# Delta-rule block inverses: 32x32 substitution against 16x16 substitution joined by TensorE products, with a new order of the woven streams

## The chip, the cores and the metric

The kernel runs on one core of one Trainium2 chip. The metric is the device time of one execution in microseconds, the median of the runs that are shown. The engines are named as in the profile: PE (TensorE, products), PEld (its weight loads), DVE (VectorE), ACT (ScalarE), POOL (GpSimd) and SP (SyncE, which issues nearly all DMAs of this kernel).

## What is computed

Two layers of a diffusion backbone over 512 latent tokens with 256 context tokens, 1024 features, everything in float32. Layer 0 mixes tokens in two ways side by side, neighbourhood attention (8 heads of 64) and a gated delta rule in both directions (4 heads of 128); layer 1 mixes with a gated spatial unit. Each is followed by a squared-ReLU MLP. The delta rule is the part at hand. The kernel works with blocks of 128 tokens (2 of context, 4 of latent tokens), in which the reference does this:

```python
kk = jnp.einsum('nbhrd,nbhjd->nbhrj', kb, kb)
lmat = jnp.where(strict, bb[..., :, None] * kk * decay, 0.0)
rhs = jnp.concatenate([bb[..., None] * vb, (bb * eg)[..., None] * kb], axis=-1)
sol = lax.linalg.triangular_solve(lmat, rhs, left_side=True, lower=True, unit_diagonal=True)
u_v, w_k = sol[..., :dv], sol[..., dv:]
...
def step(S, xs):
    u_v_n, w_k_n, aqk_n, qg_n, kdec_n, gl_n = xs
    u = u_v_n - jnp.einsum('bhck,bhkv->bhcv', w_k_n, S)
    o = jnp.einsum('bhck,bhkv->bhcv', qg_n, S) + jnp.einsum('bhcj,bhjv->bhcv', aqk_n, u)
    S = gl_n[..., None, None] * S + jnp.einsum('bhck,bhcv->bhkv', kdec_n, u)
    return S, o
```

The kernel forms the inverse Z of the unit triangular matrix of each block instead of solving, and applies it in the scan. Per pair of heads (a group g, 0 or 1) there are 6 blocks, 2 heads and 2 directions: 24 matrices of 128x128.

## The kernel before

**Products.** A float32 product is made of three: each operand is split into a rounded part and the rest (`whi` and `wlo` for weights, `hh` and `hl` for activations), and `mm3` (lines 134 to 136) issues hi·hi, hi·lo and lo·hi into one PSUM tile. Small products of the delta rule and of attention run in plain float32. Weights come as tiles of 512 KB, one after the other, from `wall` (line 79, and line 521 in layer 0); ACT rounds them, and POOL or DVE makes the rest.

**The woven stage.** `start` (manual order) computes the modulation, the norm and the first three projection tiles. Then `even_mixer` hands 33 generators, the streams, to `weave` (lines 451 to 481). A stream emits some instructions and yields an engine with an assumed duration. `weave` keeps one clock for each of PE, ACT, DVE and POOL and always resumes the stream whose time is the earliest; times up to PE's clock count as equal, and among equals the first in the list wins. So the list is an order of priority. What comes out is one fixed program order for each engine and for SP, and each engine works its queue in that order. Streams wait for each other through events (`signal`, `wait`) and for buffers through tokens (`take`, `give`); tags name buffers: `pd`, `pt`, `pg` in PSUM, `c`, `y`, `g`, `k`, `h`, `a` in SBUF.

The streams that matter here: `dense` projects the 26 tiles that `start` leaves over (PSUM tile `pl` for latent tokens, `pc` for context); `dn_keys`, `dn_values`, `dn_queries` convolve, normalise, rotate and transpose; `dn_matrices(g)` forms the strictly triangular N of each block (line 897) and stores it in `nd` (line 904); `dn_base(g)` inverts the diagonal 32x32 blocks; `dn_inverses(g)` joins them to 64 and to 128 in 6 steps; `dn_scan(g)` runs the recurrence over the steps, and scan 1 waits for scan 0; `dn_outputs` and `dn_finish` make the outputs; `att_keys`, `att_values`, `att_queries` store attention's operands to DRAM; `att_heads` loads a head's operands (`khh`, `kll`, `kcc`, `qhl`: lines 1314 and 1315) when four `k` or four `h` buffers are free; four `attention` lanes work 32 units of 128 queries (lines 1337 to 1377, the last writes `oat`); `ada_woven` makes later modulations on DVE; `out_first` starts the output projection.

**`dn_base` before** puts the 96 diagonal 32x32 blocks of a group on 112 partitions (forward ones on 0 to 47, backward ones on 64 to 111, which are transposed on the way in), and substitutes row by row, 31 rows, the m-th with a product and a reduction over m x m elements on each partition:

```python
for r in range(30, -1, -1):
    m = 31 - r
    nc.vector.tensor_tensor(out=tmp[:, 0:m, 0:m], in0=Z[:, r + 1:32, r + 1:32].rearrange("p j c -> p c j"),
                            in1=nb[:, r, r + 1:32].unsqueeze(1).to_broadcast([112, m, m]), op=ALU.mult)
    nc.vector.tensor_reduce(out=Z[:, r, r + 1:32], in_=tmp[:, 0:m, 0:m], axis=AX.X, op=ALU.add)
```

These are lines 932 and 935 (`zt<-zs,nb` and `zs<-zt` in the profile). A transposed copy follows (938), then 4 stores to DRAM (941, 942) and 24 loads (955) that bring the blocks into `zb`, in the layout of the joins: `zq`, `zn` and `zt`.

**`dn_inverses` before.** A step loads the off-diagonal parts of N (`nm`: lines 979 to 983), lets POOL place the blocks on the diagonals of W and Z (line 990, by a product with the mask `lmask`), multiplies N by W on PE (1009), copies to SBUF on ACT (1011), multiplies by the narrow `zn` (1014), and DVE copies the off-diagonal 32-blocks into Z (1018). The second half of a step (1024 to 1044) joins 64-blocks in the same manner; line 1024 transposes Z on PE. The scan applies Z in line 1112.

## Time and profile before

| | us |
|---|---|
| median of 3 runs (1743.1 to 1745.63) | 1744.21 |
| the profiled execution, its own time | 1746.16 |
| its span, first to last instruction | 1744.3 |
| PE busy (94% of the span) | 1640.8 |
| DVE busy (57%) | 1001.1 |
| ACT busy (35%) | 615.1 |
| POOL busy (14%) | 241.3 |

Busy time counts how long an engine had an instruction in work. PE's instructions overlap, so PE can be called busy and still be slow: the granted clock (PEclk) is given as a share of 2.4 GHz, and 0.5 is 1.2 GHz. The woven stage lies between about 85 us and 537 us of the span.

### The profile page before, as it was taken

What the parts mean: (1) busy time and instruction counts of PE and PEld (TensorE: products, weight loads), DVE (VectorE), ACT (ScalarE), POOL (GpSimd) and SP (SyncE); (2) the same over time, 40 slices, a digit from 0 to 9 for tenths busy, and PEclk for the clock granted to TensorE, in tenths of its full rate; (3) what the DMA queues carried; (4) which work ended last, traced back from release to release, by engine and by line L of the source; (5) the groups of instructions that cost most, each with busy time, mean ns of one, the idle gap of its engine ahead of it and who ended that gap; (6) DMA issues with size and microseconds to landing.
All of it is one profiled execution on the core that took longest, in us unless ns stands there. A gap on an engine that the chain in (4) does not pass through costs nothing.

```text
span 1744.3 us, 23500 instructions
## 1 busy us (share of the span) xinstructions
PE 1640.8 (94%) x8845; PEld 1393.5 (80%) x8845; DVE 1001.1 (57%) x2082; ACT 615.1 (35%) x1002; POOL 241.3 (14%) x215
## 2 busy tenths in 40 slices
PE   7889887969888999999999999999999999999997
PEld 4678776858877888888888999888888888888886
DVE  7876999655756865566646334535444744234433
ACT  4575342336532542123324332323223443123321
POOL 3433344535202100000002000000000200000000
PEclk9999998989879999999999999999999999999999
DMA  9147553676754355555542323232222233233322
GB/s 335 39 131 215 188 171 94 183 215 205 201 170 132 133 193 193 187 188 194 188 137 74 95 86 122 85 97 85 86 87 93 65 105 97 97 97 97 97 87 71
DMA packets 122182, 236.19 MB, mean 135 GB/s; under 512 B 38178, under 2 KB 60114, under 8 KB 122068
## 3 DMA queue, kind: packets, MB, share of 16 engines
q1 hardware_dynamic: 121780, 234.51, 42.1%
q8 instruction: 70, 1.15, 0.3%
q14 instruction: 44, 0.36, 0.1%
q10 hardware_dynamic: 288, 0.17, 0.0%
HBM read 212.59 MB, written 22.04 MB: 135 GB/s over the span
## 4 chain that ended last, share of the span: by engine, by line
PE 78%; DVE 13%; issue 2%; ACT 2%; DMA 2%; SPq 1%; POOL 1%; DVEq 0%; ACTq 0%; POOLq 0%
PE po L134 10%; PE po L135 10%; PE po L136 10%; PE pf L135 9%; PE pf L136 9%; PE pf L134 9%; PE pv L1703 3%; PE pv L1704 3%; PE pv L1705 3%; DVE zt L932 2%; PE tP L1374 2%; DVE junk L334 2%; PE pm L1736 1%; DVE zs L935 1%; PE S L1343 1%
## 5 line engine op out<-in xcount | busy, mean ns | idle before, releaser
L86 ACT CAST whi<-wraw 128x1024 fp32r<-128x1024 f32 x203 | 213.0, 1049 | 642.5 <-PE po L135 355.3
L87 DVE TENSOR_TENSOR wlo<-wraw,whi 128x1024 fp32r<-128x1024 f32 x189 | 231.6, 1225 | 323.1 <-ACT whi L86 305.0
L135 PE MATMUL pf<-nl,whi 128*128 128x512 f32 (+1 forms) x736 | 278.0, 378 | 3.1 <-DVE nl L210 3.1
L136 PE MATMUL pf<-nh,wlo 128*128 128x512 f32 (+1 forms) x736 | 276.8, 377 | 0.9 <-POOL wlo L87 0.9
L134 PE MATMUL pf<-nh,whi 128*128 128x512 f32 (+1 forms) x736 | 277.1, 378 | 0.1
L134 PE MATMUL po<-mh,whi 128*128 128x512 f32 (+1 forms) x544 | 207.5, 381 | 0.0
L136 PE MATMUL po<-mh,wlo 128*128 128x512 f32 (+1 forms) x544 | 207.4, 381 | 0.0
L135 PE MATMUL po<-ml,whi 128*128 128x512 f32 (+1 forms) x544 | 207.2, 381 | 0.0
L87 POOL TENSOR_TENSOR wlo<-wraw,whi 128x1024 fp32r<-128x1024 f32 x14 | 33.4, 2383 | 1148.8 <-ACT whi L86 1141.9
L135 PEld LDWEIGHTS pf<-nl,whi 128*128 128x128 f32 x736 | 138.7, 188 | 28.8 <-DVE nl L210 4.3
L136 PEld LDWEIGHTS pf<-nh,wlo 128*128 128x128 f32 x736 | 138.4, 188 | 25.6 <-POOL wlo L87 1.0
L134 PEld LDWEIGHTS pf<-nh,whi 128*128 128x128 f32 x736 | 138.1, 188 | 24.6 <-ACT whi L86 0.3
L134 PEld LDWEIGHTS po<-mh,whi 128*128 128x128 f32 x544 | 102.0, 187 | 22.3
L135 PEld LDWEIGHTS po<-ml,whi 128*128 128x128 f32 x544 | 102.0, 187 | 22.2
L136 PEld LDWEIGHTS po<-mh,wlo 128*128 128x128 f32 x544 | 101.9, 187 | 22.0
L1704 PE MATMUL pv<-whi,nl 128*128 128x256 f32 x384 | 108.3, 284 | 1.6 <-DVE nl L210 1.6
L1703 PE MATMUL pv<-whi,nh 128*128 128x256 f32 x384 | 108.0, 284 | 1.1 <-ACT nh L209 1.1
L1705 PE MATMUL pv<-wlo,nh 128*128 128x256 f32 x384 | 108.1, 283 | 0.0
L1592 DVE SCALAR_TENSOR_TENSOR xr<-po,gt,xr 128x512 f32<-128x512 f32 (+1 forms) x54 | 37.1, 690 | 115.0 <-PE po L136 114.9
L134 PE MATMUL pl<-hh,whi 128*128 128x512 f32 x232 | 97.9, 422 | 4.4 <-DVE ycv L570 2.6
L528 POOL TENSOR_TENSOR wlo<-wraw,whi 128x1024 fp32r<-128x1024 f32 x31 | 77.9, 2515 | 161.3 <-ACT whi L526 158.4
L135 PE MATMUL pl<-hl,whi 128*128 128x512 f32 x232 | 93.7, 404 | 1.1 <-POOL hl L359 1.1
(373 smaller groups left out, 3121.8 us busy)
## 6 DMA issues: line engine op xcount, KB each, us to landing
wraw<-in_wall_dram SPq DMA_DIRECT2D x237, 512.0 KB
araw<-in_adat_dram SPq DMA_DIRECT2D x80, 512.0 KB
kvt<-kvd SPq DMA_DIRECT2D x24, 256.0 KB
scraw<-in_ada_dram SPq DMA_DIRECT2D x16, 256.0 KB
E<-gd SPq DMA_DIRECT2D x12, 256.0 KB
nd<-N SPq DMA_DIRECT2D x24, 128.0 KB
x<-in_x_dram SPq DMA_DIRECT2D x8, 256.0 KB
shraw<-in_adat_dram SPq DMA_DIRECT2D x4, 512.0 KB
```

Source lines behind the costliest of these rows:

```text
L86: self.nc.scalar.copy(out=hi, in_=w)
L87: (engine or self.split_engine).tensor_tensor(out=lo, in0=w, in1=hi.bitcast(F32), op=ALU.subtract)
L134: self.nc.tensor.matmul(out=out, lhsT=wh, rhs=hh, start=(first and i == 0), stop=False)
L135: self.nc.tensor.matmul(out=out, lhsT=wh, rhs=hl, start=False, stop=False)
L136: self.nc.tensor.matmul(out=out, lhsT=wl, rhs=hh, start=False, stop=(last and i == n - 1))
L334: nc.vector.tensor_tensor_reduce(out=junk, in0=wsh[k][i], in1=row, scale=1.0, scalar=0.0, op0=ALU.mult, op1=ALU.add, accum_out=sa[:, k, i, ...
L528: self.nc.gpsimd.tensor_tensor(out=lo, in0=w, in1=hi.bitcast(F32), op=ALU.subtract)
L932: nc.vector.tensor_tensor(out=tmp[:, 0:m, 0:m], in0=Z[:, r + 1:32, r + 1:32].rearrange("p j c -> p c j"), in1=nb[:, r, r + 1:32].unsqueeze ...
L1592: self.nc.vector.scalar_tensor_tensor(out=self.x[m][:, c0:c1], in0=ps, scalar=gate[:, m:m + 1], in1=self.x[m][:, c0:c1], op0=ALU.mult, op1 ...
L1703: nc.tensor.matmul(out=ps, lhsT=hh, rhs=wh, start=(k == 0), stop=False)
L1704: nc.tensor.matmul(out=ps, lhsT=hl, rhs=wh, start=False, stop=False)
L1705: nc.tensor.matmul(out=ps, lhsT=hh, rhs=wl, start=False, stop=(k == KD - 1))
```

## The change

The substitution stops at 16x16 blocks: `dn_base` keeps both 16-blocks of each 32-block on the same partition, does 15 rows over two m x m squares at once, and stores one array, `zd`. It reads this back in two halves, makes the transposes with DVE's transpose of 32x32 blocks, and joins the 16-blocks to 32x32 with two rounds of 12 narrow products on PE (16 columns each), between them a placing on the diagonals by a DVE product with a mask. The off-diagonal 16x16 parts of N come by 8 loads into `n16`, which is cleared once at the start. ACT and DVE copy the result into `zb`, where 24 loads did it before. N is stored by direction in `nd`, 256 columns a row.

`dn_inverses` places nothing on POOL any more. Z lies in two fixed tiles `zz`, cleared once; POOL clears two 32x32-blocks in each step; the first product takes the narrow `zt`, DVE places its result with the mask `beside32`, and ACT copies the diagonal blocks of Z.

In the planner, many assumed durations are raised, an instruction no longer starts before its stream's own time, the hop between engines is 0.2 instead of 0.15, and DMA issues by the streams go through a helper `dma` that counts 0.45 us of SP's queue for each. The list of streams is in another order. There are 8 `g` buffers instead of 10, 2 `zb` instead of 1, and a smaller DMA scratch. Inverses of group 1 wait in the plan for those of group 0. Left out of the diff below are further changes of assumed durations and calls of `nc.sync.dma_start` that became `self.dma`, the lines that leave `dn_base`, and the old list of streams (both stand in the code above).

```diff
-NSTEP = 8 * (16 * 512 + 16)
+NSTEP = 8 * (16 * 256 + 16)
...
-        hop = 0.15
+        hop = 0.2
         clock = dict.fromkeys("PADG", 0.0)
         self.events = {}
+        self.queue = 0.0
...
+            t = max(t, self.t)
...
             live[best][1] = t + d
+
+    def dma(self, out, in_):
+
+        self.queue = self.t = max(self.queue, self.t)
+        self.queue += 0.45
+        return self.nc.sync.dma_start(out=out, in_=in_)
...
-        ndt = self.dram.tile([6 * NSTEP], F32, name=f"nd{g}")
-        nd = [bass.AP(ndt.tensor, ndt.offset + n * NSTEP, [[512, P], [1, 512]]) for n in range(6)]
+        ndt = self.dram.tile([12 * NSTEP], F32, name=f"nd{g}")
+        nd = lambda t, dd: bass.AP(ndt.tensor, ndt.offset + t * NSTEP + dd * P, [[256, P], [6 * NSTEP, 2], [1, P]])
...
     def dn_base(self, g):
         nc = self.nc
         nd = yield from self.wait(("nd", g))
         for _ in range(3):
             yield from self.take("a")
...
+        mk = lambda n: self.raw.tile([P, 1024], F32, name=n, tag="a")
+        zd = self.dram.tile([96, 1024], F32, name=f"zd{g}")
+        work, Z, spare = mk("nb"), mk("zs"), mk("zt")
+        b16 = lambda t: t.rearrange("p (s a b) -> p s a b", s=2, b=16)
+        nb, tmp, raw = b16(work[0:112, 0:512]), b16(work[0:112, 512:1024]), b16(spare[0:112, 0:512])
+        bw = slice(64, 112)
+        n0 = nd(0, 0)
+        for t, p0, dd, n in ((raw, 64, 1, 48), (nb, 0, 0, 48), (nb, 48, 0, 16)):
+            src = bass.AP(n0.tensor, n0.offset + dd * P, [[32 * 256 + 32, n], [16 * 256 + 16, 2], [256, 16], [1, 16]])
+            self.dma(out=t[p0:p0 + n], in_=src)
         nc.gpsimd.memset(Z, 0.0)
...
+        nc.gpsimd.memset(Z[:, 0:1024:33], 1.0)
         yield "G", 1.0
+        beside = lambda r, c, dd: bass.AP(n0.tensor, n0.offset + dd * P + r * 256 + c, [[256, 16], [NSTEP, 12], [1, 16]])
+        for b in range(0, P, 32):
+            f, e = slice(b, b + 16), slice(b + 16, b + 32)
+            self.dma(out=self.n16[f, :, e], in_=beside(b, b + 16, 0))
+            self.dma(out=self.n16[e, :, f], in_=beside(b + 16, b, 1))
         yield "", 2.0
...
+        nc.scalar.copy(out=nb[bw], in_=raw[bw].rearrange("p s a b -> p s b a"))
+        yield "A", 0.6
+        za = Z[0:112]
+        zd16 = bass.AP(za.tensor, za.offset, [za.ap[0], [528, 2], [32, 16], [1, 16]])
+        for r in range(14, -1, -1):
+            m = 15 - r
+            nc.vector.tensor_tensor(out=tmp[:, :, 0:m, 0:m], in0=zd16[:, :, r + 1:16, r + 1:16].rearrange("p s j c -> p s c j"),
+                                    in1=nb[:, :, r, r + 1:16].unsqueeze(2).to_broadcast([112, 2, m, m]), op=ALU.mult)
+            yield "D", 0.12 + m * m / 480
+            nc.vector.tensor_reduce(out=zd16[:, :, r, r + 1:16], in_=tmp[:, :, 0:m, 0:m], axis=AX.X, op=ALU.add)
+            yield "D", 0.12 + m * m / 480
+        self.dma(out=zd[0:48], in_=Z[0:48])
+        self.dma(out=zd[48:96], in_=Z[bw])
+        yield "", 2.2
+        v = lambda t, o: t[:, o:o + 384].rearrange("p (i t c) -> p i t c", i=2, c=32)
+        w16 = lambda t: t.rearrange("p (i t c) -> p i t c", i=2, c=16)
+        d0, d1, t0, t1 = v(work, 0), v(work, 384), v(spare, 0), v(spare, 384)
+        zt16, zn16 = w16(work[:, 768:960]), w16(spare[:, 768:960])
+        for o, dd in ((d0, 0), (t1, 1)):
+            for i in range(2):
+                src = bass.AP(zd.tensor, zd.offset + (2 * dd + i) * 24 * 1024, [[32, P], [4096, 6], [1, 32]])
+                self.dma(out=o[:, i], in_=src)
+        yield "", 2.5
+        fl = lambda t: t.rearrange("p i t c -> p (i t c)")
+        nc.vector.transpose(out=fl(t0), in_=fl(d0))
+        nc.vector.transpose(out=fl(d1), in_=fl(t1))
+        yield "D", 1.0
+        a, b = slice(0, 16), slice(16, 32)
+        nc.vector.tensor_tensor(out=zt16, in0=t0[..., a], in1=t1[..., b], op=ALU.add)
+        nc.vector.tensor_tensor(out=zn16, in0=d0[..., b], in1=d1[..., a], op=ALU.add)
+        yield "D", 0.71
+        yield from self.take("zb")
+        zb = self.pool.tile([P, 1536], F32, name="zb", tag="zb", bufs=2)
+        zq = zb[:, 0:768].rearrange("p (x i t c) -> p x i t c", i=2, x=2, c=32)
+        zn, zt = v(zb, 768), v(zb, 1152)
+        y = yield from self.tp("y16", "pt")
+        y1, y2 = w16(y[:, 0:192]), w16(y[:, 192:384])
+        for i in range(2):
+            for t in range(6):
+                nc.tensor.matmul(out=y1[:, i, t], lhsT=self.n16[:, i * 6 + t], rhs=zt16[:, i, t], start=True, stop=True)
+            yield "P", 1.35
+        h16 = slice(0, 64), slice(64, P)
+        for x in range(2):
+            for h in range(2):
+                nc.scalar.copy(out=zq[h16[h], x], in_=(d1, d0)[(x + h) % 2][h16[h]])
+        yield "A", 2.0
+        for i in range(2):
+            w = Z[:, 0:768].rearrange("p (t s c) -> p t s c", t=6, c=16)
+            nc.vector.tensor_tensor(out=w, in0=y1[:, i].unsqueeze(2).to_broadcast([P, 6, 8, 16]),
+                                    in1=self.beside16.rearrange("p (s c) -> p s c", c=16).unsqueeze(1).to_broadcast([P, 6, 8, 16]),
+                                    op=ALU.mult)
+            yield "D", 0.9
+            for t in range(6):
+                nc.tensor.matmul(out=y2[:, i, t], lhsT=Z[:, t * P:(t + 1) * P], rhs=zn16[:, i, t], start=True, stop=True)
+            yield "P", 1.35
+        for x in range(2):
+            for h in range(2):
+                dd = 1 - (x + h) % 2
+                z = zq[h16[h], x, :, :, (b, a)[dd]]
+                nc.vector.scalar_tensor_tensor(out=z, in0=y2[h16[h]], scalar=self.row16[h16[h], dd:dd + 1], in1=z,
+                                               op0=ALU.mult, op1=ALU.add)
+        yield "D", 1.2
+        self.give("pt")
         for _ in range(3):
...
+            self.give("a")
+        for k in range(4):
+            ks = slice(k * 32, (k + 1) * 32)
+            x = (1, 0, 0, 1)[k]
+            nc.scalar.copy(out=zn[ks], in_=zq[ks, 1 - x])
             for i in range(2):
...
+                nc.vector.transpose(out=zt[ks, i].rearrange("p t c -> p (t c)"), in_=zq[ks, x, i].rearrange("p t c -> p (t c)"))
+        yield "D", 2.4
+        self.signal(("zb", g), (zq, zn, zt), 0.3)
...
         zq, zn, zt = yield from self.wait(("zb", g))
-        zq = zq.rearrange("p i x f -> p (i x) f")
-        bd = self.lmask.rearrange("p (b c) -> p b c", c=32)
-
-        def place(o, z, n):
-            nc.gpsimd.tensor_tensor(out=o.rearrange("p (s b c) -> p s b c", s=n, c=32), in0=z.unsqueeze(2).to_broadcast([P, n, 4, 32]),
-                                    in1=bd.unsqueeze(1).to_broadcast([P, n, 4, 32]), op=ALU.mult)
+        beside = self.beside32.rearrange("p (b c) -> p b c", c=32).unsqueeze(1).to_broadcast([P, 2, 4, 32])
         two = lambda t: t.rearrange("p (i f) -> p i f", i=2)
+        if g > 0:
+            yield from self.wait(("inverses", g - 1))
         N = yield from load(0)
         for t in range(6):
             nxt = (yield from load(t + 1)) if t < 5 else None
-            ts = slice(t * 32, (t + 1) * 32)
             yield from self.take("Z")
-            Z = yield from self.tu("Z", "g")
+            Zv = self.zz[t % 2]
+            for x, b, c in ((0, 3, 2), (1, 2, 3)):
+                nc.gpsimd.memset(Zv[b * 32:(b + 1) * 32, :, x, c * 32:(c + 1) * 32], 0.0)
+            yield "G", 0.3
             W = yield from self.tu("W", "g")
-            place(W[:, 0:256], zt[:, :, ts], 2)
-            yield "G", 0.7
-            place(Z, zq[:, :, ts], 4)
-            yield "G", 1.4
-            Zv = Z.rearrange("p (i x f) -> p i x f", i=2, x=2)
             y = yield from self.tp("y", "pg")
             sl = lambda o, i: slice(o + i * P, o + (i + 1) * P)
             for i in range(2):
-                nc.tensor.matmul(out=y[:, sl(0, i)], lhsT=N[:, 0, i], rhs=W[:, sl(0, i)], start=True, stop=True)
+                nc.tensor.matmul(out=y[:, 32 * i:32 * i + 32], lhsT=N[:, 0, i], rhs=zt[:, i, t], start=True, stop=True)
             yield "P", 0.43
-            nc.scalar.copy(out=W[:, 256:512], in_=y[:, 0:256])
-            yield "A", 0.27
+            nc.vector.tensor_tensor(out=W[:, 256:512].rearrange("p (i b c) -> p i b c", i=2, c=32),
+                                    in0=y[:, 0:64].rearrange("p (i c) -> p i c", i=2).unsqueeze(2).to_broadcast([P, 2, 4, 32]),
+                                    in1=beside, op=ALU.mult)
+            yield "D", 0.42
+            for b in range(4):
+                ps = slice(b * 32, (b + 1) * 32)
+                nc.scalar.copy(out=Zv[ps, :, :, ps], in_=zq[ps, :, :, t].rearrange("p x i c -> p i x c"))
+            yield "A", 1.0
             for i in range(2):
-                nc.tensor.matmul(out=y[:, 256 + 32 * i:288 + 32 * i], lhsT=W[:, sl(256, i)], rhs=zn[:, i, ts], start=True, stop=True)
+                nc.tensor.matmul(out=y[:, 256 + 32 * i:288 + 32 * i], lhsT=W[:, sl(256, i)], rhs=zn[:, i, t], start=True, stop=True)
             yield "P", 0.43
             for x, b, c in ((1, 0, 1), (1, 3, 2), (0, 2, 3), (0, 1, 0)):
                 ps = slice(b * 32, (b + 1) * 32)
                 nc.vector.tensor_copy(out=Zv[ps, :, x, c * 32:(c + 1) * 32], in_=two(y[ps, 256:320]))
-            yield "D", 0.5
+            yield "D", 0.9
...
+        self.signal(("inverses", g))
...
-            yield "P", 0.86
-            self.give("g")
+            yield "P", 0.9
...
-        self.lmask = self.const.tile([P, P], F32, name="lmask")
+        self.beside16, self.beside32 = [self.const.tile([P, P], F32, name=f"beside{n}") for n in (16, 32)]
+        self.row16 = self.const.tile([P, 2], F32, name="row16")
+        self.n16 = self.const.tile([P, 12, P], F32, name="n16")
+        self.zz = [self.const.tile([P, 2, 2, P], F32, name=f"zz{i}") for i in range(2)]
         self.nm = [self.pool.tile([P, 2, 2, P], F32, name=f"nm{i}", tag=f"nm{i}", bufs=1) for i in range(2)]
-        for t in self.nm:
+        for t in self.nm + self.zz + [self.n16]:
             nc.gpsimd.memset(t, 0.0)
         o = P
...
-        count = dict(pd=0, pt=2, pg=0, w=2, whi=3, a=1, h=0, k=0, bm=2, zb=1, Z=2, kv=2, nr=2,
+        count = dict(pd=0, pt=2, pg=0, w=2, whi=3, a=1, h=0, k=0, bm=2, zb=2, Z=2, kv=2, nr=2,
...
+        self.weave([self.weights(), self.dn_finish(0), self.dn_keys(1), self.attention(3, L), self.dn_inverses(0),
+                    self.dn_outputs(1), self.dn_gates(), self.dn_scan(0), self.dn_keys(0), self.dn_values(0), self.dn_values(1),
+                    self.dn_matrices(0), self.dn_base(0), self.dn_scan(1), self.att_keys(), self.release_h(), self.att_values(),
+                    self.att_gates(), self.att_finish(), self.out_first(), self.dn_finish(1), self.dn_base(1),
+                    self.att_queries(), self.attention(2, L), self.dn_queries(1), self.dn_outputs(0), self.dn_queries(0),
+                    self.dn_matrices(1), self.load_residual(), self.attention(0, L), self.attention(1, L), self.dn_inverses(1),
+                    self.att_heads(), self.dense(), self.ada_woven()])
...
-            self.phase(ctx, {"c": 7, "y": 6, "k": 10, "sc": 2, "g": 10, "ar": 2, "tri": 1, "cos": 1, "sin": 1}, {"pd": 3, "pt": 2, "pg": 3})
+            self.phase(ctx, {"c": 7, "y": 6, "k": 10, "sc": 2, "g": 8, "ar": 2, "tri": 1, "cos": 1, "sin": 1}, {"pd": 3, "pt": 2, "pg": 3})
...
-    lm = [(a == b).astype(f)]
+    s, u = i[:, None] // 16, i[None, :] // 16
+    even = (i[:, None] // 16 % 2 == 0).astype(f)
+    lm = [((s ^ 1) == u).astype(f), ((a ^ 1) == b).astype(f), even, f(1) - even]
...
-    nc = bacc.Bacc("TRN2", target_bir_lowering=False, num_devices=1)
+    nc = bacc.Bacc("TRN2", target_bir_lowering=False, num_devices=1, dynamic_dma_scratch_size=1024)
```

## Rows read from the trace of the kernel before

**Rows 1.** The page, busy us of an engine, share of the span, instructions.

```profile
PE 1640.8 (94%) x8845; PEld 1393.5 (80%) x8845; DVE 1001.1 (57%) x2082; ACT 615.1 (35%) x1002; POOL 241.3 (14%) x215
```

**Rows 2.** Busy time by stage: us; PE, PEld, DVE, ACT, POOL; PEclk, DMA share, GB/s.

```profile
85.00:180.00 95.00, 87.72 (x513) 75.38 (x513) 65.82 (x172) 57.54 (x94) 35.89 (x22) 0.98 0.54 168
180.00:300.00 120.00, 97.81 (x526) 82.66 (x525) 113.86 (x224) 40.51 (x68) 44.77 (x32) 0.91 0.50 148
300.00:350.00 50.00, 47.85 (x337) 42.47 (x337) 34.55 (x82) 18.16 (x52) 29.77 (x36) 1.00 0.60 184
350.00:375.00 25.00, 10.48 (x58) 8.76 (x57) 8.76 (x29) 6.05 (x13) 4.89 (x6) 0.73 0.71 202
375.00:455.00 80.00, 77.42 (x593) 71.83 (x592) 52.27 (x186) 42.79 (x107) 39.53 (x58) 1.00 0.73 210
455.00:537.00 82.00, 67.96 (x363) 60.28 (x362) 54.30 (x168) 35.31 (x76) 9.74 (x12) 0.75 0.65 191
537.00:1744.30 1207.30, 1185.44 (x6139) 1007.69 (x6137) 605.07 (x1090) 373.09 (x530) 41.47 (x19) 1.00 0.35 115
```

**Rows 3.** Groups by line, 80 to 660 us: busy us, mean ns, idle before.

```profile
L932 DVE TENSOR_TENSOR zt<-zs,nb 112x1 f32<-112x1 f32 (+30 forms) x62 | 55.3, 892 | 1.3
...
L935 DVE TENSOR_REDUCE zs<-zt 112x1 f32<-112x1 f32 (+30 forms) x62 | 30.9, 499 | 1.3
...
L990 POOL TENSOR_TENSOR Z<-zb,lmask 128x512 f32<-128x512 f32 x12 | 15.7, 1308 | 0.2
```

**Rows 4.** Timeline of PE: start us, us, instruction, idle before and its releaser.

```profile
285.52 0.66 PE L1024 MATMUL y<-ident,Z 128*128 128x128 f32 x2 [7.45 <-DVE Z L1018]
```

**Rows 5.** The substitution: its lines (ns min/median/max, first and last start), timelines of DVE and POOL.

```profile
L932 DVE TENSOR_TENSOR zt<-zs,nb x62: 149/726/3607, 178.8 to 319.1; 112x1 f32<-112x1 f32 x2, 112x4 f32<-112x4 f32 x2, 112x9 f32<-112x9 f32 x2, 112x16 f32<-112x16 f32 x2
L935 DVE TENSOR_REDUCE zs<-zt x62: 154/419/1153, 179.3 to 325.2; 112x1 f32<-112x1 f32 x2, 112x2 f32<-112x4 f32 x2, 112x3 f32<-112x9 f32 x2, 112x4 f32<-112x16 f32 x2
...
205.64 1.01 DVE L932 TENSOR_TENSOR zt<-zs,nb 112x441 f32<-112x441 f32 x1
...
245.87 1.15 DVE L935 TENSOR_REDUCE zs<-zt 112x31 f32<-112x961 f32 x1
...
278.54 2.35 POOL L528 TENSOR_TENSOR wlo<-wraw,whi 128x1024 fp32r<-128x1024 f32 x1 [5.69 <-ACT whi L526]
...
279.15 2.43 DVE L932 TENSOR_TENSOR zt<-zs,nb 112x441 f32<-112x441 f32 x1
```

**Rows 6.** PE's waits, 80 to 660 us; two links of the chain that ended last.

```profile
PE S L1343 <- DMA qhl<-qad: 11.1, 1, 11.1
...
104.79 3.83 DMA E<-gd
...
407.82 0.89 PE ks L1102 x8
```

**Rows 7.** Timeline of SP's DMA issues: start us, us, issue.

```profile
335.57 6.11 SPq L955 DMA_DIRECT2D zb<-zn  x8
...
348.77 0.92 SPq L955 DMA_DIRECT2D zb<-zn  x2
```

**Rows 8.** The first transfer of the heads: ns min/median/max, first and last issue.

```profile
L1314 SPq DMA_DIRECT2D khh<-kad x16: 445/587/656, 359.2 to 484.2; - x16
```

**Rows 9.** Ends of attention units, 455 to 537 us, in the same form.

```profile
L1377 DVE TENSOR_SCALAR oat<-tP,sm x17: 278/284/285, 459.1 to 522.3; 128x64 f32<-128x64 f32 x17
```

**Rows 10.** Prices of like instructions: a group by line; others in the form of rows 5.

```profile
L1178 DVE TENSOR_TENSOR odn<-au,kk 128x256 f32<-128x256 f32 x8 | 3.0, 420 | 5.3 <-PE au L1166 3.9 <-PE pc L135 1.4
...
L1032 ACT COPY W<-y x12: 372/372/373, 288.0 to 452.5; 128x256 f32<-128x256 f32 x12
...
L1014 PE MATMUL y<-zb,W x48: 194/276/402, 277.4 to 447.6; 128*128 128x32 f32 x48
...
L1560 POOL MEMSET nm<- x2: 524/524/524, 0.7 to 1.2; 128x512 f32 x2
```

More of the change, by code (lines that the diff above doesn't have):

```diff
@@ L948, in dn_base @@
-        zq = zb[:, 0:768].rearrange("p (i x f) -> p i x f", i=2, x=2)
-        zn, zt = [zb[:, o:o + 384].rearrange("p (i f) -> p i f", i=2) for o in (768, 1152)]
-        def load(o, z, dd, p0, n):
-            for i in range(2):
-                src = bass.AP(z.tensor, z.offset + (2 * dd + i) * 24 * 1024 + p0 * 32, [[32, n], [4096, 6], [1, 32]])
-                nc.sync.dma_start(out=o[p0:p0 + n, i].rearrange("p (t c) -> p t c", c=32), in_=src)
-        for x in range(2):
-            for half in range(2):
-                load(zq[:, :, x], zc[0], 1 - (half + x) % 2, half * 64, 64)
@@ L1065, in load @@
             for dd in range(2):
[L1066 removed]
+                self.dma(out=kvt[:, dd], in_=self.kv[g][order[dd][t]].rearrange("p (a f) -> p a f", a=2))
             return kvt
@@ L1550, in out_first @@
             self.give("h")
+        self.signal("done")
     def even_mixer(self):
```

243 lines of the change are left out of this document (105 added, 138 removed).

## Prediction

> **What bounds the kernel now.** I read the page first, for the whole. PE is busy for 94% of the span [rows 1], so a change that is not about dense products can win only where PE stands still or runs slowly. The second view, busy time by stage, says where that is [rows 2]. From 537 us on (both MLPs and the gated mixer) PE is busy for 1185 of 1207 us at full clock, and the diff touches nothing there. The first 85 us are the start, untouched but for memsets and constants. The change lives in the woven stage between: 452 us, of which PE is busy for 389. The 63 us of idle PE lie like this: 7 in 85 to 180, 22 in 180 to 300, 2 in 300 to 350, 15 in 350 to 375, 3 in 375 to 455, 14 in 455 to 537.
>
> To that comes the granted clock: 0.91 in the second stage, 0.73 in the fourth, 0.75 in the last. The time at 1.2 GHz is twice what is missing to 1 (22, 14 and 41 us), and work that is done in it at 1.2 GHz would take half as long at 2.4. In the last stage PE is busy for 83% of the time, so some 17 of the 41 us are lost; in the second about 6, in the fourth and the first 2 each. Idle and slow PE together cost **about 89 us of 452**: 9, 28, 2, 16, 3 and 31, stage by stage. That is all that the change can win, less what it adds to PE.
>
> What ends the waits: from 180 to 300 VectorE (DVE) is busy for 114 of 120 us [rows 2], and 86 us in all are the block substitution, lines 932 and 935 [rows 3]. PE's longest stall there shows what this does: the transpose y<-Z at 285.52 waited 7.45 us for the copies of line 1018 [rows 4], which stood in DVE's queue behind substitution steps, one of 2.43 us among them [rows 5]. From 350 to 375 PE waits 11.1 us for qhl, the last transfer of the first attention head [rows 6]. It was issued late: SP had first spent 14 us on 24 issues for zb, eight in 6.11 us and then about 0.46 each, up to 349.7 [rows 7], and the head's first transfer left at 359.2 [rows 8]. After 455 little but attention is left: 17 of its 32 units end there, between 459 and 523 [rows 9], with PE at 1.2 GHz for half of the stage.
>
> **The change part by part.** *Substitution on DVE.* Line 932 takes 0.15 us for one element and 1.01 for 441: 0.15 us and 1.95 ns an element. Line 935 takes 0.15 for one and 1.15 for 961: 1.04 ns an element [rows 5]. Two 16-blocks side by side keep the transposed read, so I keep both prices. Fifteen rows with 2m² elements are 2480 elements instead of 10416: 15 x 0.15 + 4.8 = 7.1 us and 15 x 0.15 + 2.6 = 4.8, so 11.9 a group where rows 3 show 43.1; the transposing copy goes too (1.1, by line 935's 961 elements). New on DVE in each group: two 32x32-block transposes of 384 columns, two adds of 192, two products of 768, four updates of 192 and eight transposes of 192 on 32 partitions. Scaled from 0.42 us for 256 columns [rows 10] they are 0.55, 0.35, 0.95, 0.35 and 0.3 each: 7.5 us. (If a transpose paid line 932's price, 0.9 instead of 0.55, it would be 1 us more; it reads one tensor, so I take the lower.) That makes 19.4 for 44.2: **25 us less a group, 50 in both**. The inverses get one more DVE product of 256 columns in each of 12 steps, 0.42 each: 5 us back. DVE has 148 us of work between 180 and 350; 45 less, and it is no longer full.
>
> The slow forms deserve a second look: 441 elements took 1.01 us at 205.64 and 2.43 at 279.15, while POOL ran wlo from 278.54 to 280.89 [rows 5]. The Trainium skill (SBUF — State Buffer, Who interferes with whom) says that a DVE instruction with two SBUF inputs and a GpSimd instruction that reads SBUF block each other on a shared read interface; this trace agrees. By that rule up to 1.4 us falls on each product that meets a wlo, and with two or three such in a group the saving would be 21 to 23 instead of 25.
>
> *POOL* loses the placing of line 990, 15.7 us for Z [rows 3] and half as much for W, and gets 24 memsets of 128 columns, 0.2 each beside 0.52 for 512 [rows 10]. *ACT* gets four copies of 32 partitions a step (0.25 each beside 0.37 for 256 columns [rows 10]: 12 us) and eight larger ones a group (0.4: 6 us), and loses the 12 copies of line 1011 and half of line 928: some 12 us more. It is busy for 200 of 452 us [rows 2] and hides them; were it full, they would stand in the steps' chain, 1 us a step. *SP*: 33 issues a group (5 loads, 4 stores, 24 for zb) become 17 (3 loads, 8 of n16, 2 stores, 4 reads): at 0.46 that is 7.4 us less a group. The 64-byte rows of n16 are only 1536 a group and land during the substitution, before whose end nobody needs them; without that cover they cost one landing, 3.8 us.
>
> *PE* gets 24 narrow products a group. Four fp32 products of 128 columns run in 0.89 us, as eight instructions [rows 6], and an instruction with 32 columns shows the same 0.28 [rows 10]. So 0.22 each: **10.6 us more PE**; 21 at 1.2 GHz. Were columns what counts it would be under 3, but rows 10 speak for the higher.
>
> *The chain.* Today 30 us pass from the last reduction of group 0 (247.0) to the second inverse product (277.4) [rows 5, 10]. New: a store and a read, each at most a landing like E's 3.83 us [rows 6], transposes and adds 1.8, products 1.3, placing 1, products, placing and products 2.7, updates 1.4, transposes 2.4: some 18 us. And the substitution, 68 us from first to last step because its 43 us stand between other DVE work [rows 5], should take 20 to 25. The inverses of group 0 can begin some 50 us sooner, those of group 1 more; scan 0 ends sooner, and with it come the five k buffers of which the first head needs four.
>
> *At nothing:* memsets of zz and n16 (2.7 us by rows 10, on POOL in its first 16 us, before wlo; later they would delay a wlo by as much), two more constant loads on SP's slack at 37 us, nd stored as two half rows, ten g buffers to eight (Z takes none any more), a second zb, the scratch size, since the page lists hardware queues alone. The planner's new costs move instructions only; an order nearer to the real durations saves stalls like the 7.45 us, which no row prices.
>
> **The sum.** Stage by stage: the early 9 stay; 28 becomes 10, because DVE stops being full; 16 becomes 7, as SP's stretch halves and buffers come sooner but some fetch stays exposed; 31 becomes 19: heads that begin 40 us sooner finish seven more units under other work at 5.3 us each (15 of them in 375 to 455), so that ten remain alone, at 4 us. 18 + 9 + 12 = 39, with 2 for fewer stalls 41, less 10.6: **30 us**. From the profiled 1746.2 us (the span of 1744.3 and 1.9 around it) to 1716; the median of the runs shown lies 2 us lower, so 1714.
>
> **Rivals.** *A, attention spreads wholly.* If scan 0 ends near 300, half of the heads run under projections; the last stage loses 25 of its 31, the fourth 16, the second 22: 63 less 10.6 is 52, so 1692. For it: after 375, with other work beside it, PE idles for only 3 of 80 us. Against: the last heads need the last projections.
>
> *B, the idle only moves.* If the first head still leaves at 359 [rows 8], because its buffers or the order let it no sooner, the projections run out sooner and attention stands alone sooner, at 1.2 GHz. Then the 18 of the second stage are won, the 10.6 paid and some 5 given back: 1742.
>
> *C, slower.* PE takes its queue in order, and the joining sets three new hand-offs a group (products behind adds, then twice behind a placing) and one changed in each of 12 steps on DVE: 18 places where the 7.45 us of rows 4 can come again, 8.5 with a slow start after it. Four cancel the 30; with six it is 1714 + 51 = 1765. For it: DVE keeps other work in its queue. Against: what stood before line 1018 there is now a third as long.
>
> **How the numbers follow.** My forecast (1695 to 1732: PE's 10.6 or 21, all or nothing of the tail's 12) gets 0.50, A 0.20, B 0.15, C 0.15. A measurement of this kernel can tell about 0.2%, 3.5 us, from no change; half of B lies within, 0.08, the rest of B is faster: 0.77 faster, 0.15 slower. The range from 1682 to 1749 leaves out the far part of A and nearly all of C.
>
> **What would show it.** Right: the substitution's lines near 24 us instead of 86, DVE under 85% where it was 95%, inverses that begin before 240, a first S before 340, fewer than 13 units alone, 96 narrow instructions at 0.11 us. Wrong: PE waits of 5 us or more for the joining's DVE steps, a first S after 355, or a last stage whose clock stays at 0.75.

## The result, and the profile after

The changed kernel takes 1720.15 us, median of 4 runs (1719.23 to 1721.98), beside 1743.65 us for the kernel before (4 runs, 1742.96 to 1745.63): a ratio of 0.9865, with a 95% interval of 0.9848 to 0.9882. That is 23.5 us faster, where 30 were forecast. The two profiled executions lie further apart, 1746.16 and 1719.23 us; their spans are 1744.3 and 1717.4, so 26.9 us are to be found in the traces.

The page of the changed kernel, busy us of an engine, share of the span, instructions:

```profile
PE 1641.4 (96%) x8941; PEld 1396.2 (81%) x8941; DVE 965.3 (56%) x2064; ACT 631.8 (37%) x1056; POOL 218.0 (13%) x218
```

PE does as much as in [rows 1] in a shorter span. Busy time by stage of the changed kernel, columns as in [rows 2]. The last projection now ends at 389 us and the woven stage at about 509, so the limits are moved there:

```profile
85.00:180.00 95.00, 86.35 (x489) 73.85 (x490) 63.43 (x161) 57.34 (x93) 33.86 (x21) 0.95 0.54 161
180.00:300.00 120.00, 110.03 (x651) 95.79 (x650) 93.27 (x235) 53.59 (x109) 44.23 (x47) 0.93 0.59 171
...
300.00:350.00 50.00, 48.81 (x323) 43.16 (x321) 36.50 (x111) 17.76 (x47) 16.08 (x21) 1.00 0.84 274
350.00:389.00 39.00, 38.61 (x267) 34.96 (x268) 27.96 (x92) 26.06 (x61) 13.69 (x18) 1.00 0.78 219
389.00:455.00 66.00, 55.26 (x428) 50.72 (x427) 38.26 (x136) 38.00 (x96) 23.62 (x46) 0.95 0.81 230
455.00:509.00 54.00, 51.42 (x323) 46.61 (x323) 31.12 (x99) 21.92 (x55) 8.66 (x10) 0.87 0.31 100
509.00:1717.40 1208.40, 1185.44 (x6135) 1006.77 (x6133) 608.60 (x1100) 374.51 (x532) 39.06 (x18) 0.99 0.34 115
```

The woven stage fell from 452 us to 424; what follows it takes 1208 us, as before. From 180 to 300 us DVE is busy for 78% of the time, where it was 95%. To count both kernels in one way, I take for the loss of a stage its idle PE time and, for the slow clock, busy time x (1 - clock):

| loss of PE, us | before | after |
|---|---|---|
| 85 to 180 | 9.0 | 13.0 |
| 180 to 300 | 31.0 | 17.7 |
| 300 to 375 (after: to 389) | 19.5 | 1.6 |
| from there to the end of the woven stage | 33.6 | 22.8 |
| sum | 93.1 | 55.1 |

So 38 us of loss went, and the stage is 28 shorter: the rest, 358.9 to 368.9, is 10 us of added work on PE. Groups of the changed kernel by line, 80 to 660 us (busy us, mean ns, idle before):

```profile
L952 DVE TENSOR_TENSOR nb<-zs,nb 112x2 f32<-112x2 f32 (+14 forms) x30 | 19.7, 656 | 0.5
...
L955 DVE TENSOR_REDUCE zs<-nb 112x2 f32<-112x2 f32 (+14 forms) x30 | 9.6, 321 | 0.5
...
L986 PE MATMUL y<-nb,n 128*128 128x16 f32 x48 | 5.9, 262 | 0.1
...
L1000 PE MATMUL y<-zt,zs 128*128 128x16 f32 x48 | 5.6, 256 | 0.0
```

The substitution is 29.3 us where [rows 3] have 86.2, and the narrow products are 96 instructions in 11.5 us, 0.12 each. PE's waits in the changed kernel, 80 to 560 us (total us, times, longest):

```profile
PE tvac L590 <- DVE vaTc L1297: 5.4, 2, 3.7
...
PE pu L1170 <- DVE zz L1100: 2.5, 3, 1.3
...
PE y L1081 <- DVE zz L1075: 1.9, 2, 1.3
...
PE y L1071 <- DVE W L1062: 1.5, 3, 0.7
```

The longest is 3.7 us. The wait of 11.1 us for qhl [rows 6] and that of 7.45 us for line 1018 [rows 4] are gone, and the hand-offs from DVE to PE in inverses and scan (the last three rows) cost 6 us in eight waits.

### The profile page after: what moved, and what is told of

It is laid out like the page before. It is cut to its first block, busy times and chain, and to the rows that moved or that the text cites. A ratio compares the mean times of both kernels' runs of the same rounds, so it can differ in the third digit from the quotient of the medians.

```text
span 1717.4 us, 23655 instructions
## 1 busy us (share of the span) xinstructions
PE 1641.4 (96%) x8941; PEld 1396.2 (81%) x8941; DVE 965.3 (56%) x2064; ACT 631.8 (37%) x1056; POOL 218.0 (13%) x218
## 4 chain that ended last, share of the span: by engine, by line
PE 69%; DVE 3%; issue 1%; ACT 0%; POOL 0%; DVEq 0%; ACTq 0%; POOLq 0%
PE po L134 10%; PE po L135 10%; PE po L136 10%; PE pf L135 9%; PE pf L136 9%; PE pf L134 9%; PE pv L1770 3%; PE pv L1771 3%; PE pv L1772 3%; PE pm L1803 1%; PE tP L1431 0%; DVE nl L210 0%; PE st L173 0%; DVE accx L201 0%; DVE modt L208 0%
## 5 line engine op out<-in xcount | busy, mean ns | idle before, releaser
L87 DVE TENSOR_TENSOR wlo<-wraw,whi 128x1024 fp32r<-128x1024 f32 x189 | 231.5, 1225 | 324.8 <-ACT whi L86 306.4
L87 POOL TENSOR_TENSOR wlo<-wraw,whi 128x1024 fp32r<-128x1024 f32 x14 | 33.4, 2384 | 1149.3 <-ACT whi L86 1131.1
L134 PE MATMUL pl<-hh,whi 128*128 128x512 f32 x232 | 102.2, 441 | 2.9 <-DVE ycv L578 2.9
L136 PE MATMUL pl<-hh,wlo 128*128 128x512 f32 x232 | 95.7, 412 | 0.0
```

What stands on the lines that cost most here:

```text
L87: (engine or self.split_engine).tensor_tensor(out=lo, in0=w, in1=hi.bitcast(F32), op=ALU.subtract)
L134: self.nc.tensor.matmul(out=out, lhsT=wh, rhs=hh, start=(first and i == 0), stop=False)
L136: self.nc.tensor.matmul(out=out, lhsT=wl, rhs=hh, start=False, stop=(last and i == n - 1))
```

## The experiments

The kernels ran on three chips, each beside runs of the kernel before, so they are compared by their ratio to it. "To after" is (ratio - 0.9865) x 1743.65 us; an interval is some 3 us to either side, 5 to 7 for e5, e7, e8 and e12; the 3 us of the changed kernel's own ratio come on top.

One thing has to be known before these runs are read: the plan of `weave` is not the last word on the order of instructions. e3, e4, e6 and e10 change no assumed duration, so they have the plan of the kernel that they start from. Their traces still show PE, ACT and DVE working in another order in places, with DVE instructions moved by up to 12 places in e6, 35 in e3 and e10 and 57 in e4; what moves them is not shown. Only e9 (beside the changed kernel) and e11 (beside e8) ran exactly the order of the kernel that they are compared with.

| run | what | median us | ratio (95% interval) | to after, us |
|---|---|---|---|---|
| e1_math_only | new inverses, old order | 1723.41 | 0.9878 (0.9861 to 0.9894) | +2 |
| e2_plan_only | old inverses, new order | 1758.12 | 1.0079 (1.0064 to 1.0094) | +37 |
| e3_dve_back | after, DVE work put back | 1759.95 | 1.0085 (1.0070 to 1.0100) | +38 |
| e4_dve_cut | before, DVE work taken out | 1726.18 | 0.9899 (0.9882 to 0.9916) | +6 |
| e5_dve_back_planned | e3, known to the plan | 1762.99 | 1.0108 (1.0076 to 1.0140) | +42 |
| e6_pe_double | narrow products twice | 1742.60 | 0.9997 (0.9976 to 1.0017) | +23 |
| e7_late_plan | inverses 30 us later in plan | 1715.05 | 0.9847 (0.9805 to 0.9889) | -3 |
| e8_wlo_dve | wlo on DVE | 1704.40 | 0.9771 (0.9741 to 0.9802) | -16 |
| e9_pool_back | POOL's placing put back | 1730.53 | 0.9929 (0.9908 to 0.9950) | +11 |
| e10_sp_back | 16 issues a group put back | 1746.36 | 1.0000 (0.9982 to 1.0019) | +24 |
| e11_wlo_both | e8, and POOL reads the same | 1726.13 | 0.9899 (0.9883 to 0.9916) | +6 |
| e12_wlo_late | e8 and e7 | 1704.19 | 0.9774 (0.9748 to 0.9800) | -16 |

**The inverses or the order?** The diff does two things, and the prediction gave the new order nothing. e1 has the new `dn_base`, `dn_inverses`, buffers and constants under the old list and durations; e2 is its complement. The core of e1 against the changed kernel (the list of streams and the other streams' durations go back in the same way):

```diff
-        hop = 0.2
+        hop = 0.15
...
-        self.queue = self.t = max(self.queue, self.t)
-        self.queue += 0.45
...
-            yield "A", 1.05
+            yield "A", 0.95
```

> The 16x16 substitution with its joining, the new buffers and copies, but the old list of streams, the old assumed durations, the hop of 0.15 and no clock for SP's queue. Theory M (the gain comes from less DVE work in the substitution and a shorter way to the inverses, as the prediction has it): most of the gain is here, 10 to 24 us faster than before, with DVE in 180 to 300 us well under 95%. Theory O (the gain comes from the new order and the planner's truer durations, the substitution only allows it): within 8 us of before, or slower, because the order was found for the old durations.

> The old 32x32 substitution, old inverses and old buffers, with the new list of streams, the raised durations, the hop of 0.2 and the clock for SP's queue. Theory M: less than 8 us faster than before, or slower, because DVE is still full while the substitution runs (86 us of it). Theory O: 10 to 24 us faster than before.

e1 alone is 21 us faster than before, with DVE busy for 75% of the time from 180 to 300 us, and the order adds some 2 us, which the intervals do not part from nothing. The new order with the old inverses is 14 us slower than before. Its two largest waits of PE, 80 to 560 us:

```profile
PE tqT L590 <- DVE qtok L621: 14.2, 1, 14.2
PE y L1032 <- DVE Z L1026: 13.2, 5, 10.4
```

Both are waits for DVE, the second at the place of the 7.45 us of [rows 4], and DVE is busy for 110 of the 120 us from 180 to 300. This fits an order that brings other work forward and meets a DVE that is still full; that it makes the whole 14 us is not shown. Theory O is out.

**DVE's load alone, from both sides.** e3 gives DVE back about as much work as the change took; e4 takes the long rows out of the old substitution and edits nothing else.

```diff
# e3, behind each of the 15 reductions
+            sq = self.cos[0:112, 0:441].rearrange("p (j c) -> p c j", c=21)
+            for _ in range(2):
+                nc.vector.tensor_tensor(out=spare[0:112, 512:953].rearrange("p (c j) -> p c j", c=21), in0=sq, in1=sq, op=ALU.mult)
# e4, before both instructions of a row of the old substitution
+            if m < 16:
# e5: e3, and the plan knows
-            yield "D", 0.12 + m * m / 480
+            yield "D", 2.12 + m * m / 480
```

> The changed kernel in its own order, with two extra DVE products of 441 elements behind each of the 15 substitution steps of a group (about 30 us more DVE work a group, about what the change took away; nobody uses their results). Theory M: most of the gain is lost, 12 to 25 us slower than the changed kernel. Theory O: less than 8 us slower, since the order leaves the time for it.

> The kernel before in its own order, with the substitution's first-long 16 of 31 rows (m of 16 and more) left out, about 35 us less DVE work a group; nothing else moves, the 24 loads into zb and the placing on POOL stay. What it leaves out are rows 0 to 15 of each 32x32 inverse. Theory M: 12 to 25 us faster than before. Theory O: less than 8 us faster.

> As e3_dve_back, but the plan knows of the extra DVE work (2.0 us more assumed in each of the 15 steps), so that the program order is made for it. Theory M1 (what counts is DVE's time: its other work and the inverses come later whatever the order): still 15 us or more slower than the changed kernel. Theory M2 (what counted in e3 was that an order written for short steps met long ones, so that PE stood behind them in its queue): under 8 us slower than the changed kernel, or equal to it.

e4 is 17.6 us faster than before, though its 24 loads and its POOL work stay: the substitution's two lines fell from 86.2 to 19.1 us. The second inverse product of group 0 also comes 20 us sooner (257.0 us instead of 277.4), so e4 alone does not part DVE's time from an earlier inverse; e7 below does.

e3 loses the whole gain and more, but half of its extra work is not where it was meant to be. The extra products need no result of a reduction, and those of group 0 ran long before the substitution. The extra products and the reductions, in the form of [rows 5]; DVE's time with the extra products in two stretches; and busy time from 85 to 130 us, in e3 and then in the changed kernel, columns as in [rows 2]:

```profile
L958 DVE TENSOR_TENSOR zt<-cos x60: 986/1099/3210, 69.1 to 317.8; 112x441 f32<-112x441 f32 x60
...
L955 DVE TENSOR_REDUCE zs<-nb x30: 134/276/622, 200.6 to 316.1; 112x2 f32<-112x2 f32 x2, 112x4 f32<-112x8 f32 x2, 112x6 f32<-112x18 f32 x2, 112x8 f32<-112x32 f32 x2
```

```profile
85.00:130.00 45.00, 30.78 (x23) 0.81 0.23 71
...
180.00:300.00 120.00, 27.90 (x21) 0.90 0.56 159
```

```profile
85.00:130.00 45.00, 29.48 (x169) 24.51 (x169) 44.69 (x70) 22.14 (x39) 12.72 (x5) 0.81 0.23 71
...
85.00:130.00 45.00, 41.28 (x238) 35.34 (x239) 33.93 (x78) 34.56 (x59) 16.04 (x8) 0.96 0.40 129
```

The products took 1.3 us each, not 1.0, 80 us in all, and cost 38. The 30 of group 0 lie between 69 and 128 us, ahead of that group's substitution, whose first reduction comes at 200.6 us instead of 180.3. DVE is full there, and PE's loss from 60 to 130 us, counted as in the table of losses, is 30 us where the changed kernel has 11: about half of the 38. Only the other half stands for the 30 products of group 1, from 250 to 319 us, beside a substitution. In e5, with the work known to the plan, the first 30 lie as early (70 to 128 us) and cost as much there, and the rest is some 23 us: M2 is out, since that rest alone is far above 8 us. So a full DVE holds PE up in either place; that the substitution's stage is where the change gained rests on e4, on e1 beside e2, and on the second half of e3 and e5.

**The way to the inverses.** The prediction priced a shorter chain from the substitution to the first inverse.

```diff
-        self.signal(("zb", g), (zq, zn, zt), 0.3)
+        self.signal(("zb", g), (zq, zn, zt), 30.0)
```

> The joined blocks are signalled 30 us later in the plan (30.0 instead of 0.3), so that the inverses of both groups, and what hangs on them, are put 30 us later into the queues; no instruction is added. Theory C (an early inverse is a part of the gain by itself): 8 us or more slower than the changed kernel. Theory D (DVE's freed time is the gain, and the way to the inverses is short enough either way): within 5 us of the changed kernel.

Not slower: if anything 3 us faster, within its interval. The first inverse product comes at 277.4 us instead of 247.4, but the order then catches up: the sixth step of group 0 begins 7 us later than in the changed kernel and the last of group 1 9 us sooner. So 30 us at the start of the inverses cost nothing as long as the plan knows it, and theory C is out.

**The price of the joining on PE.**

```diff
+                for _ in range(2):
-                nc.tensor.matmul(out=y1[:, i, t], lhsT=self.n16[:, i * 6 + t], rhs=zt16[:, i, t], start=True, stop=True)
+                    nc.tensor.matmul(out=y1[:, i, t], lhsT=self.n16[:, i * 6 + t], rhs=zt16[:, i, t], start=True, stop=True)
# and the same for y2
```

> Each of the 24 narrow fp32 products of a group that join 16-blocks is issued twice, in the same order otherwise. Theory P (the prediction's term: PE's added work counts in full): 10 to 12 us slower than the changed kernel. Rival (it lies in time in which PE would be idle anyway, waiting for the placing of the joining): under 4 us.

23 us, twice what I expected. The lines of the doubled products, 80 to 600 us, and then busy time in the two stages from 240 us on, columns as in [rows 2]:

```profile
L1002 PE MATMUL y<-zt,zs 128*128 128x16 f32 x96 | 15.8, 312 | 0.0
L987 PE MATMUL y<-nb,n 128*128 128x16 f32 x96 | 14.0, 294 | 0.9 <-DVE nb L975 0.9
```

```profile
240.00:300.00 60.00, 54.71 (x306) 47.93 (x306) 43.72 (x108) 24.41 (x55) 23.69 (x27) 0.87 0.46 124
300.00:350.00 50.00, 50.00 (x311) 46.90 (x311) 28.28 (x75) 14.89 (x39) 13.73 (x23) 0.84 0.53 177
```

The lines grew from 11.5 to 29.8 us, so 18 for the doubling: part of it ran at 1.2 GHz (24 instructions took 2.75 us at 234.5 us and 22 took 4.71 at 239.3), and the granted clock is 0.87 and 0.84 where the changed kernel has 0.97 and 1.00. The other 5 us are not assigned. Nothing of it is hidden, so the rival is out; but theory P's 10 to 12 us are missed as well, and 23 is near the price that the prediction has for 1.2 GHz, 21.

**SP and POOL put back.** e10 issues 16 small loads a group where 24 stood before; e9 does the two placings of line 990 again, into a scratch tile.

```diff
# e10, behind the read-back of zd
+        for k in range(16):
+            p0, o = k % 4 * 32, k // 4 * 192
+            src = bass.AP(zd.tensor, zd.offset + k // 4 * 24 * 1024 + p0 * 32, [[32, 32], [4096, 6], [1, 32]])
+            nc.sync.dma_start(out=self.scr[p0:p0 + 32, o:o + 192].rearrange("p (t c) -> p t c", c=32), in_=src)
# e9, in each step of the inverses, for n = 2 and 4
+                nc.gpsimd.tensor_tensor(out=self.scr[:, 0:n * P].rearrange("p (s b c) -> p s b c", s=n, c=32),
+                                        in0=zq[:, :, :, t].rearrange("p x i c -> p (x i) c")[:, 0:n].unsqueeze(2).to_broadcast([P, n, 4, 32]),
+                                        in1=bd.unsqueeze(1).to_broadcast([P, n, 4, 32]), op=ALU.mult)
```

> The changed kernel in its own order, with 16 small loads a group put back on SP where the blocks are read back (into a scratch tile that nobody reads), 7.4 us more of SP's queue a group by the prediction's price. Theory R (SP's stretch of issues is a part of the gain, the prediction's 16 to 7 in the stage that waited for the first head): 4 to 10 us slower than the changed kernel. Rival (with the heads no longer the next thing in SP's queue it is hidden): within 3 us.

> The changed kernel in its own order, with the two POOL products that the change took out of each step of the inverses put back as extra work (256 and 512 columns into a scratch tile that nobody reads, 12 times each, some 25 us of POOL in all). Theory Q (the placing on POOL cost something, because DVE instructions that meet a POOL product are held up): 4 to 12 us slower than the changed kernel. Rival (POOL is off every path that sets the end, 13% busy): within 3 us.

e10 costs 24 us, far above both theories. SP's issues and one DVE product of e10, and then the same store and product in the changed kernel (start us, us, instruction):

```profile
217.84 8.07 SPq L972 DMA_DIRECT2D scr<-zd  x16
...
283.33 8.69 SPq L972 DMA_DIRECT2D scr<-zd  x15
...
333.33 0.69 DVE L756 TENSOR_TENSOR A<-A,kq 128x512 f32<-128x512 f32 x1
...
334.04 0.32 SPq L489 DMA_DIRECT2D ad<-A  x1
...
368.62 0.48 SPq L489 DMA_DIRECT2D khh<-kad  x1
```

```profile
308.48 0.68 DVE L756 TENSOR_TENSOR A<-A,kq 128x512 f32<-128x512 f32 x1
...
309.18 0.32 SPq L489 DMA_DIRECT2D ad<-A  x1
```

The loads take 8 to 9 us a group (7.4 by the prediction's price), 17 in both. But the first head's khh leaves at 368.6, where the changed kernel issues it at 340.4. Most of the 28 us is one stand: SP's queue waits from 312.0 to 334.0 us to store A, whose product DVE did at 333.3 instead of 308.5, because it stands behind other work in DVE's queue, which ran in another order here. PE then waited 6.0 us for qhl again, and between 350 and 400 us it was busy for 36 of 50 us at a clock of 0.76 (48.5 at 1.00 in the changed kernel). So the 24 us hold the issues and an order that moved with them, and what the issues cost by themselves stays open. e4 bears on it: there all 24 loads stay, and khh still leaves at 345.3 us, 14 of the 19 us sooner that the change brought.

e9, in the changed kernel's own order, costs 11 us. Its largest wait of PE, and POOL's timeline up to its end:

```profile
PE pu L1175 <- POOL zz L1099: 8.6, 1, 8.6
```

```profile
302.45 6.29 POOL L1056 TENSOR_TENSOR scr<-zb,beside 128x512 f32<-128x512 f32 x5
308.71 2.82 POOL L536 TENSOR_TENSOR wlo<-wraw,whi 128x1024 fp32r<-128x1024 f32 x1
311.49 7.43 POOL L1056 TENSOR_TENSOR scr<-zb,beside 128x256 f32<-128x256 f32 x6
318.98 0.29 POOL L1098 COPY W<-zz 64x128 f32<-64x128 f32 x1
319.35 0.29 POOL L1099 COPY zz<-zz 64x128 f32<-64x128 f32 x1
```

POOL is 14% busy over the span and still holds the scan here: a copy of 0.29 us, for which the scan's product waits, stands behind 16.5 us of placings and a wlo. The plan does not know of the added products, and crowds them more than the old kernel would, so 11 us is an upper bound of what the placing cost. The rival in which POOL costs nothing is out.

**Who holds DVE up.** Two timelines of the changed kernel, POOL and DVE:

```profile
187.54 2.40 POOL L536 TENSOR_TENSOR wlo<-wraw,whi 128x1024 fp32r<-128x1024 f32 x1 [5.38 <-ACT whi L534]
...
203.66 2.40 POOL L536 TENSOR_TENSOR wlo<-wraw,whi 128x1024 fp32r<-128x1024 f32 x1 [4.00 <-ACT whi L534]
```

```profile
187.68 2.48 DVE L952 TENSOR_TENSOR nb<-zs,nb 112x162 f32<-112x162 f32 x1
...
204.10 2.00 DVE L148 SCALAR_TENSOR_TENSOR rst<-rst,ssq 128x8 f32<-128x8 f32 x1
...
211.02 0.16 DVE L148 SCALAR_TENSOR_TENSOR rst<-rst,ssq 128x8 f32<-128x8 f32 x1
...
253.62 0.45 DVE L952 TENSOR_TENSOR nb<-zs,nb 112x162 f32<-112x162 f32 x1
```

The same 162 elements take 0.45 us alone and 2.48 beside a wlo, and even 8 columns take 2.00 instead of 0.16: such an instruction, with two inputs in SBUF, that meets a wlo stands until about its end. There are 31 of these wlo on POOL, so e8 forms them on DVE, and e11 lets POOL read the same two tensors as well.

```diff
# e8
-            self.nc.gpsimd.tensor_tensor(out=lo, in0=w, in1=hi.bitcast(F32), op=ALU.subtract)
-            yield "G", 2.5
+            self.nc.vector.tensor_tensor(out=lo, in0=w, in1=hi.bitcast(F32), op=ALU.subtract)
+            yield "D", 1.22
# e11: e8, and before the yield
+            for o in (0, 512):
+                self.nc.gpsimd.tensor_tensor(out=self.scr, in0=w[:, o:o + 512], in1=hi.bitcast(F32)[:, o:o + 512], op=ALU.subtract)
```

> In the woven stage the rest of the weights (wlo, 31 times) is formed on DVE, where one takes 1.2 us, instead of on POOL, where one takes 2.4 us and a DVE instruction that meets it takes about 2 us longer in the trace of the changed kernel. Theory S (each of these pairs holds DVE up for as long as DVE would need for the work itself): the same as the changed kernel or up to 15 us faster. Theory L (DVE's load decides; 38 us more of it is like e3): 10 us or more slower.

> As e8_wlo_dve, with POOL reading the same two tensors for the same result once more, in two halves into a scratch tile that nobody reads, so that DVE still meets POOL products as often as in the changed kernel and has the 39 us of wlo besides. Theory S (e8 was faster because DVE was no longer held up by POOL's products): 15 us or more slower than e8, at least as slow as the changed kernel. Rival (e8 was faster because wlo was ready sooner, 1.2 instead of 2.4 us, or because its order happens to be better): within 6 us of e8.

> e8_wlo_dve and e7_late_plan together: wlo on DVE, and the joined blocks signalled 30 us later in the plan. If the two gains are of separate causes (DVE held up by POOL; the order in the last stage), 3 to 8 us faster than e8. If e7's gain was one of order by chance, within 4 us of e8 either way.

e8 beats both kernels: 16 us below the changed one, 40 below the one before. Its page, and its DVE groups, 80 to 660 us:

```profile
PE 1642.1 (96%) x8941; PEld 1398.3 (82%) x8941; DVE 973.9 (57%) x2095; ACT 629.5 (37%) x1054; POOL 143.7 (8%) x187
```

```profile
L536 DVE TENSOR_TENSOR wlo<-wraw,whi 128x1024 fp32r<-128x1024 f32 x31 | 39.3, 1268 | 15.6 <-ACT whi L534 15.1
...
L952 DVE TENSOR_TENSOR nb<-zs,nb 112x2 f32<-112x2 f32 (+14 forms) x30 | 13.5, 451 | 3.0 <-DMA nb<-nd 2.6
L955 DVE TENSOR_REDUCE zs<-nb 112x2 f32<-112x2 f32 (+14 forms) x30 | 9.6, 319 | 0.4
```

DVE took over 39 us of work and is busy for only 8.6 us more over the span (965.3 before this edit), so all its other work became 31 us shorter; the substitution's products alone fell from 19.7 to 13.5 us. Theory L is out. With POOL's reads put back (e11) 22 us are lost again; DVE is busy for 997.0 us, 23 more than in e8 with the same instructions, and the first two of these groups are longer, 43.3 and 17.0 us. A better order is no cause of the gain, since DVE, PE, ACT and SP run in e8's order in e11, nor is a wlo that is ready sooner, since it takes 1.40 us there and 1.27 in e8. What e11 does not keep apart: its extra products also fill POOL, 103.5 us where the wlo of the changed kernel took 74.9, and hold the weight buffers longer. e12 adds nothing to e8.

## Why the prediction was right, point by point

*What bounds.* Right. The loss lay in the woven stage, and 28 us came out of it and nothing elsewhere. That DVE's load in the stage is the cause is shown by e4, by e1 against e2 and by the half of e3's extra work that lies in the stage. That the time came near the forecast is in part luck: the chain below failed, and errors of both signs cancel in the sum.

*Substitution on DVE.* The lines gave 14.7 us a group for the 11.9 forecast, the joining's DVE work 7.9 for 7.5, so 21.7 were saved and not 25. The term that was mis-sized is the products' price, and the cause is measured: in e8, with no wlo on POOL, the two lines take 11.6 a group. This is the rule of the Trainium skill (SBUF — State Buffer, Who interferes with whom) which the prediction weighed: a DVE instruction with two inputs in SBUF and a GpSimd instruction that reads SBUF exclude each other. The trace agrees, and by it the prediction had 21 to 23. I should have taken that value, and asked what else on DVE meets a wlo; that was worth 16 us (e8).

*PE's added work.* 10.6 us forecast, 11.5 in the lines and 10 in the sum over the stages. That none of it is hidden is shown by e6, which paid the dearer price, the one at 1.2 GHz.

*POOL and SP.* POOL's relief was put at nothing in the sum, and putting the placing back costs up to 11 us (e9): the prediction left out that a short copy, for which PE waits, can stand behind the long instructions in POOL's queue. SP's stretch was the reason given for 9 us, together with buffers that come sooner; the stages from 300 to 389 gave 18. In e4, with all of SP's loads kept, the first head leaves 14 us sooner, so most of this came with DVE's relief; SP's own share stays open (e10). The costs of putting parts back, 38, 24 and 11, sum to more than the gain, so they are no shares of it.

*The chain.* This step failed. I expected 18 us from the last reduction to the first inverse product; it is 211.8 to 247.4 in group 0, 36 us, more than the 30 before. Timelines of the changed kernel, DVE and PE:

```profile
221.01 0.34 DVE L976 TENSOR_TENSOR zt<-nb 128x192 f32<-128x192 f32 x1
...
239.52 2.57 DVE L1017 STREAM_TRANSPOSE zb<-zb 32x192 f32<-32x192 f32 x8
```

```profile
224.51 1.41 PE L986 MATMUL y<-nb,n 128*128 128x16 f32 x12
226.54 1.53 PE L986 MATMUL y<-nb,n 128*128 128x16 f32 x12
231.54 1.41 PE L1000 MATMUL y<-zt,zs 128*128 128x16 f32 x12
234.30 1.41 PE L1000 MATMUL y<-zt,zs 128*128 128x16 f32 x12
247.38 0.53 PE L1060 MATMUL y<-zb,nm 128*128 128x32 f32 x4
```

The store and the read took the 8 us that I had given them. But each link waits its turn between dense products, which I left out of the sum of links: DVE's adds end at 221.4 us and their products start at 224.5, the placing ends at 229.1 and its products start at 231.5, and DVE's last transposes end at 242.1, 5.3 us before the first inverse product, with PE busy all the time from 220 to 250. That is 11 of the 18 us missing. So the inverses begin 30 us sooner and not 50, at 247.4 where I wrote before 240, and the first S is at 351.9, neither before 340 nor after 355. By e7 it makes no difference, so the step was wrong, but the time did not hang on it.

*The tail.* 12 forecast, 10.8 measured, by another way. The sign of fewer than 13 units alone was wrong: 26 of the 32 units end from 388.8 us on, because the projections now end at 389 instead of 443. But they are not alone. The second scan, which was over at 455, now runs beside them until 497.5, and the clock of the last stage is 0.87 for 0.75. The seven units of the sum were to come from heads that begin 40 us sooner; the first head's khh leaves 19 us sooner. The first stage lost 4 us, which I had left unchanged.

*The rivals.* A's full spread did not come: 23 us of loss stay after 389 us. B's start of the first head did not stay at 359, it is 340.4. C's stalls did not come: no wait for the joining is over 1.3 us. The order as a cause of its own, which I gave nothing, is worth 2 us with the new inverses and minus 14 with the old ones.

*The sum.* 38 of loss less 10 of work, where I had 41 less 10.6. Early stage 4 worse, second stage 13 for 18, the next 18 for 9, the tail 11 for 12: the first two together and the third are off by 9 us each, in opposite directions. One reading of [rows 2] in the prediction was wrong: the slow clock of the second stage, counted as in the last, costs 9 us and not 6, so that its loss was 31 and not 28.

## What to carry to other kernels

Where several engines work in-order queues, look for the stage in which one of them is full and take work off it there: its other clients gain, and this is worth far more than a shorter chain to a result that the plan can also use later. Price a POOL instruction not by its own length but by what stands behind it in its queue up to the next thing that PE waits for. When work is added to test a cause, look in the trace where it ran before reading what it cost: half of e3's products ran over 70 us ahead of the substitution that they were meant for. An engine that is 14% busy can still be the one to relieve, if its long instructions hold a busy engine up: give the work to the busy one and measure.

## What the runs showed of the hardware

A POOL product of 128x1024 that reads two tensors (2.4 us) held a DVE instruction with two SBUF inputs until about its end, whatever that one's own length: 0.16 us became 2.00. Moving 31 of these to DVE, where one takes 1.27 us, added 39.3 us of work and only 8.6 us of busy time. And 96 more narrow fp32 instructions of 16 columns, 0.12 us each in the changed kernel, cost 23 us, 0.24 each, with a lower granted clock in the two stages from 240 us on (0.87 and 0.84 for 0.97 and 1.00).
